# A streaming encoder layer by fast products of seven: weight sums on VectorE instead of adding DMA, and smoother steps

## The chip, the cores and the metric

One core of a Trainium2 chip. The metric is device time in microseconds; before the change the median of three runs is 2205.09 us (2199.73 to 2208.75).

## The reference

One layer (float32), for a prompt of 512 frames and a sample of 32 frames, which share all weights; the kernel runs them as T = 544 columns.

```python
mod = silu(c) @ w_ada + b_ada                       # shift, scale, gate
h = rmsnorm(x, norm_g) * (1 + scale) + shift        # (T, 2048)
z = h @ w_in                                        # w_in (2048, 15360): 120 blocks of 128 columns
au, av, ag, lx, lg, hq, hf, hi, hg, mg = split(z)   # 8 blocks each, mg 48
ya = gmlp_mix(gelu(au), rmsnorm(gelu(av)), ws, bs) * silu(ag)   # gMLP
yb = rglru(causal_conv(lx)) * silu(lg)              # RG-LRU: gates, exp/sqrt, scan over time
yc = rmsnorm(hgrn2_scan(silu(hq), k(hf), logf(hf), hi)) * silu(hg)  # 8 heads, 128 x 128 states
out = (sig(mg0) * (ya @ wb0) + sig(mg1) * (yb @ wb1) + sig(mg2) * (yc @ wb2)) @ w_out
y = rmsnorm(x + gate * out, final_g)
```

Outputs are y and the new states of the convolution, the RG-LRU and the HGRN2 branch, and the v rows of the sample.

## The kernel before

**Products.** `z = h @ w_in` takes pairs of column blocks (b1, b2). Contraction and tokens are halved, and with the two blocks each pair is a 2 x 2 x 2 product, done by seven products instead of eight (`Group`, L330). The operands of the tokens, X1 to X7, are made once; the sums of the weights are made for each pair. Each product is an *item*: 24 matmuls of 128 x 128 by 272 columns, since each float32 weight tile is split in a high and a low part (`halved`, L308; `split`, L230: ScalarE copies to float32r, `wh`, VectorE subtracts, `wl`) and so are the tokens. 60 groups make 420 items, in the order of `todo` (L1169): four of v rows, then the 16 `head` pairs each with a `light` one (mg) behind, four light, then 16 `heavy` ones (eight gMLP, eight RG-LRU) with a light one after each four.

**Order and weight sums.** A group's products interleave with the next one's: 2, 6, 1', 5, 7', 3, 4 (a dash is the next group). Four banks of PSUM: `a` (two, alternating) and `c` (two); product 2 uses the other `a`. Of weights, b1 is halved as p0, p1 and b2 as r0, r1. Products 1, 2 and 3 use p0, p1 and r1 as loaded. Product 5 uses p0 + r0: p0 is loaded a second time and r0 is added by a DMA (`accum_op`, `load_adds`, L261). Product 7 uses q = r0 + r1, loaded and added the same way; VectorE then adds p0 for product 6 (L365), and p1 for product 4.

**Queues.** SyncE loads 512 KB tiles into rings (`raw` five, `q` two, and at the start `early` two), at most nine items ahead (`feed`, L1404). GpSimd issues the adding DMA, spills to DRAM and reloads, and computes some of the head's elementwise work. The program order is the order written by the loop at L1408: item i+2 is prepared (split, sums), item i is multiplied, its PSUM copied out, then `pump` (L453) lets each background generator take one step. A `yield` is thus one item. Every engine works through its own queue in order.

**Background.** Results are put in DRAM (`put_away`, L1122). A head (`hg_gen`, L731) runs when its four blocks are there: gates, exponentials of differences at six levels (GpSimd subtracts L789, ScalarE exponentiates, VectorE multiplies L804 and L875, TensorE multiplies L815 and L885), then states, output and norm. The first one calls `hg_setup` (L710, masks by DMA), the first RG-LRU block `lru_setup` (L1018). `y_gen` (L1191) reloads ya for the stage that follows, `merges` (L1304). Buffers of all these come from one arena, and a buffer is written again only when its last transfer has landed.

Of the kernel before, what the change touches and what calls it, by code (L numbers as in the profile page):

```python
# [42 lines left out]
RAWS = 5  # L43
# [63 lines left out]
def hybrid_step_kernel(ctx: ExitStack, tc: tile.TileContext, xT, cT, w_first, w_in, w_branch, w_out,  # L107
# [139 lines left out]
    items, loads, qloads, adds = [], [], [], []  # L247
# [6 lines left out]
    def item(prep, mul, post=None, pre=None):  # L254
        items.append((prep, mul, post, pre, len(loads), len(qloads)))

    def add(k, n, src):

        adds.append((k, n, src))

    def load_adds(i, last):  # L261

        for e in sorted(adds, key=lambda e: e[0]):
            k, n, src = e
            if k <= i and n in raws:
                nc.gpsimd.dma_start(out=raws[n], in_=src, accum_op=OP.add)  # L266
                adds.remove(e)

    at = {"load": 0, "q": 0}
    EARLY = 34  # L270
    RING = {"raw": RAWS, "early": 2, "q": 2}
# [13 lines left out]
    def load_some(upto):  # L285
        while at["load"] < min(upto, len(loads)):
            n = at["load"]
            ring = "raw"
            if n < START and n % 5 == 1:
                ring = "q"  # L290
            elif "early" in pools.open_ and n < EARLY and n % 5 == 0:
# [6 lines left out]
    def load_q(upto):  # L298
        while at["q"] < min(upto, len(qloads)):
            if at["load"] < START or not free_in("q"):  # L300
                return
            load(("q", at["q"]), qloads[at["q"]], "q", 1024)
            at["q"] += 1
# [26 lines left out]
    class Group:  # L330
# [4 lines left out]
        def __init__(self, n, b1, b2, post, posts=None):  # L335
            self.n, self.b, self.post, self.posts = n, (b1, b2), post, posts or {}
            self.w, self.raw = {}, {}
# [4 lines left out]
        def add(self, i):  # L342

            b1, b2 = self.b
            k = len(items)
            if i == 7:
                self.q = ("q", len(qloads))
                qloads.append(w_half(b2, 0))
                add(k - 5, self.q, w_half(b2, 1))
                n = self.q  # L350
            elif i in (6, 4):
                n = self.q
            else:
                n = need({1: w_half(b1, 0), 2: w_half(b1, 1), 3: w_half(b2, 1), 5: w_half(b1, 0)}[i])
                if i == 5:
                    add(k - 5, n, w_half(b2, 0))
                else:
                    self.raw[i] = n

            def prep():  # L360
                assert not any(e[1] == n for e in adds)
                self.w[i] = halved(raws[n])
                if i in (7, 6):
                    m = self.raw[1 if i == 7 else 2]
                    tt(raws[n], raws[n], raws[m], op=OP.add)  # L365
                    done[m] = True
                elif i not in (1, 2):
                    done[n] = True
# [5 lines left out]
            def after():  # L374
# [4 lines left out]
                elif i == 2:  # L379
                    self.o1 = buf()  # L380
                    tt(self.o1.ap[:, :HF], banks[self.a2], self.u1.ap, op=OP.add)
# [328 lines left out]
    def hg_setup():  # L710
# [19 lines left out]

    def hg_gen(h):  # L731
        if h == 0:
            hg_setup()
# [6 lines left out]
        nc.gpsimd.memset(qb.ap[:, 0:1], 0.0)  # L740
        yield
        yield
# [98 lines left out]
        yield  # L841
        p1, p2 = lev_mm(16), lev_mm(8)
# [9 lines left out]
        lev_w(2)  # L852
        yield
# [29 lines left out]
        nc.vector.tensor_copy(ew[:, 4:5], eq.ap[:, T:T + 1])  # L883
        p1 = lev_mm(1)
        mm(p1[:NS, 272:273], ke.ap[:, NP:], qb.ap[:, T:T + 1], start=True, stop=True)  # L885
        xs[0].free()
        zi = hbuf()
        nc.gpsimd.dma_start(out=zi.ap, in_=scratch[f"hi {h}"])
# [48 lines left out]
        nc.sync.dma_start(out=s0.ap[:, :128], in_=S0[:, h, :])  # L937
# [48 lines left out]
        newton(r, m, t)  # L986
        osb = hbuf(256)
# [6 lines left out]
        qe.free()  # L994
        yield
# [22 lines left out]
    def lru_setup():  # L1018
# [4 lines left out]
        tt(e, e, x, op=OP.min)  # L1023
        act(e, e, AF.Exp)
        ts(u2, e, 2.0, None, op0=OP.add)
# [4 lines left out]
        for n in (17, 15, 13, 11, 9, 7, 5, 3, 1):  # L1030
            tt(acc, acc, u2, op=OP.mult)
            ts(acc, acc, 1.0 / n, None, op0=OP.add)
        tt(acc, acc, u, op=OP.mult)
# [5 lines left out]
    def lru_post(b):  # L1039
# [6 lines left out]
        def post(x, lg):  # L1046
            if b == 0:
                lru_setup()
            start(lru_gen(b, x, lg, w[0]))
# [69 lines left out]
    def z_groups():  # L1119
        av = [(B_AV + j, B_AV + j + 1, av_post(j)) for j in range(0, 8, 2)]  # L1120

        def put_away(n, o, on=None):  # L1122

            if n[:2] in ("hq", "hg"):
                yield
# [14 lines left out]
        def keep(*names, on=None):  # L1140
            def post(*os):
                for n, o in zip(names, os):
                    g = put_away(n, o, on if n == names[-1] else None)
                    if n[:2] in ("hq", "hg"):
                        start(g)
                    else:
                        next(g)
# [21 lines left out]
        todo = av  # L1169
        for i in range(16):  # L1170
            todo += [head[i], light[i]]
        todo += light[16:20]
        rest = iter(light[20:])
        for i, (b1, b2, post, at_start) in enumerate(heavy):
            todo.append((b1, b2, post, {1: at_start}))
            if i % 4 == 3:
                todo.append(next(rest))
        todo += rest
        todo[-1] += ({1: lambda: start(y_gen(0, (1, 2), 0)), 2: lambda: start(y_gen(0, (1, 2), 1))},)
        groups = [Group(n, *t) for n, t in enumerate(todo)]  # L1180
        groups[0].add(1)
        groups[0].add(7)
        for n, g in enumerate(groups):
            nxt = groups[n + 1] if n + 1 < len(groups) else None
            for i in (2, 6, -1, 5, -7, 3, 4):
                if i > 0:
                    g.add(i)
                elif nxt:
                    nxt.add(-i)

    def y_gen(br, pair, h=None):  # L1191

        step = 4 if h is None else 8
        for k in range(0, 8, step):
# [6 lines left out]
            yield  # L1201
            for i, b in enumerate(bs_):
# [6 lines left out]
                if h is None or i == 3:  # L1209
# [186 lines left out]
    with tc.manual_schedule():  # L1396
# [7 lines left out]
        def feed(i):  # L1404
            load_some(items[min(i + 9, len(items) - 1)][4])
            load_q(items[min(i + 6, len(items) - 1)][5])

        for i, (_, mul, post, pre, _, _) in enumerate(items):  # L1408
            feed(i)
            load_adds(i, i + AHEAD)  # L1410
# [94 lines left out]
```

## Time and profile before

| | |
|---|---|
| median of three runs | 2205.09 us |
| profiled execution | 2206.34 us, span 2204.6 us |
| PE, PEld (weight load) busy | 2041.6 us (93%), 1945.3 us (88%) |
| DVE, ACT, POOL busy | 1282.3 (58%), 1103.0 (50%), 503.4 us (23%) |
| DMA | 412.22 MB, HBM read 363.77 MB |
| mean granted TensorE clock | 0.956 |

PE is TensorE, DVE VectorE, ACT ScalarE, POOL GpSimd, SP SyncE. Busy is the time in which an instruction runs; matmuls overlap, so one of 128 x 272 is given 295 ns although the next may start much earlier. A line number is that of the kernel; L190, L232 and L324 are helpers that many places call, and are told apart by the tile's name (`pm` the group products, `px` others, `pp` the products after).

### The profile page before, as it was taken

The page shows a single profiled execution, that of the slowest core. Times are in us where ns is not written, and L with a number is a line of the kernel's source. Part 1 is how long each engine was busy: PE and PEld are TensorE (multiplying, and loading weights), DVE is VectorE, ACT ScalarE, POOL GpSimd, SP SyncE. Part 2 cuts the span into 40 slices and gives each one's busy share as a digit, 9 for nine tenths or more (in the row PEclk, how much of TensorE's full clock was granted, in tenths as well). Part 3 has the DMA queues.
Part 4 walks back from the last instruction along what each step waited for, and adds up shares of the span by engine and source line. Part 5 has one row for each costly group of instructions (what it writes and reads, how often), then busy time and mean ns, then how long its engine had stood idle before and what let it go on. Part 6 is the DMA issues. An engine that isn't in the chain of part 4 may idle for free.

```text
span 2204.6 us, 40701 instructions
## 1 busy us (share of the span) xinstructions
PE 2041.6 (93%) x15864; PEld 1945.3 (88%) x15864; DVE 1282.3 (58%) x2204; ACT 1103.0 (50%) x2137; POOL 503.4 (23%) x720
## 2 busy tenths in 40 slices
PE   5789998989998989898999999999987999999997
PEld 3279988989898989897989999999887999999996
DVE  3365665665766575856575766678675433442226
ACT  3357544655555555554554656567565433332223
POOL 0002122232313141313133222112223222220112
PEclk8789998989999999998999999999999999999998
DMA  8977675756665666665667777666655667665554
GB/s 313 365 190 189 187 187 150 189 158 180 168 187 159 179 165 182 162 190 146 188 161 203 188 198 199 180 156 171 166 147 192 232 185 185 195 196 173 174 173 168
DMA packets 135009, 412.22 MB, mean 187 GB/s; under 512 B 16128, under 2 KB 38432, under 8 KB 134816
## 3 DMA queue, kind: packets, MB, share of 16 engines
q1 hardware_dynamic: 87408, 261.08, 35.3%
q0 software_dynamic: 41424, 138.34, 27.7%
q10 hardware_dynamic: 5984, 10.19, 1.5%
q8 instruction: 125, 2.05, 0.4%
q14 instruction: 68, 0.56, 0.1%
HBM read 363.77 MB, written 45.78 MB: 186 GB/s over the span
## 4 chain that ended last, share of the span: by engine, by line
PE 70%; DMA 8%; DVE 7%; issue 6%; ACT 6%; POOL 2%; DVEq 0%; SPq 0%; ACTq 0%; POOLq 0%
PE pm L324 41%; PE pp L324 21%; DMA q<-in_w_in_dram 3%; ACT arena L190 2%; DVE wl L232 2%; ACT wh L190 2%; PE px L815 1%; DMA d_mg<-arena 1%; PE px L1286 1%; PE px L498 1%; PE px L571 1%; DMA raw<-in_w_ss_dram 1%; DVE x L232 1%; POOL arena L789 1%; DMA arena<-d_hf 1%
## 5 line engine op out<-in xcount | busy, mean ns | idle before, releaser
L324 PE MATMUL pm<-x,wh 128*128 128x272 f32 x6720 | 1316.8, 295 | 49.2 <-ACT arena L190 22.6
L324 PEld LDWEIGHTS pm<-x,wh 128*128 128x128 f32 x6720 | 1088.8, 194 | 58.3 <-ACT arena L190 25.0
L324 PE MATMUL pm<-x,wl 128*128 128x272 f32 x3360 | 987.1, 294 | 2.4 <-DVE wl L232 2.4
L232 DVE TENSOR_TENSOR wl<-raw,wh 128x512 fp32r<-128x512 f32 x652 | 458.1, 729 | 385.0 <-ACT wh L190 381.4
L324 PEld LDWEIGHTS pm<-x,wl 128*128 128x128 f32 x3360 | 649.2, 193 | 4.4 <-DVE wl L232 4.2
L190 ACT ACTIVATE wh<-raw 128x512 fp32r<-128x512 f32 x652 | 391.4, 624 | 334.3 <-PE pm L324 238.3
L324 PE MATMUL pp<-x,wh 128*128 128x272 f32 x2560 | 487.6, 290 | 5.9 <-ACT x L190 2.6
L324 PEld LDWEIGHTS pp<-x,wh 128*128 128x128 f32 x2560 | 402.2, 189 | 20.5 <-issue 13.5
L232 DVE TENSOR_TENSOR wl<-q,wh 128x512 fp32r<-128x512 f32 x360 | 256.1, 737 | 225.9 <-ACT wh L190 224.6
L324 PE MATMUL pp<-x,wl 128*128 128x272 f32 x1280 | 369.4, 289 | 0.0
L190 ACT ACTIVATE wh<-q 128x512 fp32r<-128x512 f32 x360 | 215.5, 624 | 137.7 <-PE pm L324 98.7
L190 ACT ACTIVATE arena<-arena 128x544 f32<-128x544 f32 (+5 forms) x310 | 162.8, 554 | 209.5 <-DVE arena L1339 76.7
L324 PEld LDWEIGHTS pp<-x,wl 128*128 128x128 f32 x1280 | 241.4, 189 | 0.2 <-DVE wl L232 0.2
L190 ACT ACTIVATE arena<-pm 128x272 f32<-128x272 f32 x240 | 93.8, 391 | 182.8 <-PE pm L324 139.8
L266 POOL DMA_DIRECT2D q<-in_w_in_dram x60 | 53.5, 892 | 503.4 <-DMA q<-in_w_in_dram 184.0
L365 DVE TENSOR_TENSOR q<-q,raw 128x1024 f32<-128x1024 f32 x120 | 148.7, 1239 | 4.1
L190 ACT ACT_TABLE_LOAD x59 | 75.7, 1283 | 13.1 <-DVE arena L1063 5.3
L266 POOL DMA_DIRECT2D raw<-in_w_in_dram x60 | 54.1, 902 | 107.7 <-DMA raw<-in_w_in_dram 52.2
L789 POOL TENSOR_TENSOR arena<-arena 128x544 f32<-128x544 f32 (+1 forms) x40 | 52.6, 1327 | 60.1 <-PE px L817 18.3
L815 PE MATMUL px<-arena 128*128 128x128 f32 x160 | 32.4, 333 | 26.9 <-DVE arena L804 17.2
L1242 DVE TENSOR_TENSOR arena<-pp,arena 128x544 f32<-128x544 f32 x48 | 34.7, 723 | 37.0 <-PE pp L324 37.0
L1349 POOL TENSOR_TENSOR tail<-tail,arena 128x544 f32<-128x544 f32 (+1 forms) x15 | 18.6, 1242 | 149.5 <-ACT arena L190 149.5
(265 smaller groups left out, 1425.6 us busy)
## 6 DMA issues: line engine op xcount, KB each, us to landing
raw<-in_w_in_dram SPq DMA_DIRECT2D x240, 512.0 KB, 4.7
q<-in_w_in_dram SPq DMA_DIRECT2D x60, 512.0 KB, 5.0
q<-in_w_in_dram POOLq DMA_DIRECT2D x60, 512.0 KB, 6.3
raw<-in_w_in_dram POOLq DMA_DIRECT2D x60, 512.0 KB, 7.4
raw<-in_w_branch_dram SPq DMA_DIRECT2D x48, 512.0 KB, 4.1
raw<-in_w_ss_dram SPq DMA_DIRECT2D x44, 512.0 KB, 7.0
raw<-in_w_out_dram SPq DMA_DIRECT2D x38, 512.0 KB, 4.6
raw<-in_w_gate_dram SPq DMA_DIRECT2D x32, 512.0 KB, 4.6
```

The source lines that it names most:

```text
L190: return nc.scalar.activation(out, in_, func, **kw)
L232: tt(lo, src, hi.bitcast(F32), op=OP.subtract)
L266: nc.gpsimd.dma_start(out=raws[n], in_=src, accum_op=OP.add)
L324: mm(p, a, rhs(k, r), start=start and i == 0 and q == 0, stop=stop and i == n - 1 and q == 2, **kw)
L365: tt(raws[n], raws[n], raws[m], op=OP.add)
L498: mm(st["xss"][h][:, :HF], ones, st["sq"][q % 2][:, i, h * HF:(h + 1) * HF], start=q == 0 and i == 0, stop=q == 7 and i == 1)
L571: mm(p[32 * i:32 * i + 2, part * 256:part * 256 + 256], cs[:, 4 * q + i, :], w[:, i * 256:(i + 1) * 256], start=q == 0, stop=q == 3)
L789: ptt(v, fv(src, 0, [[2 * m, nb], [m - 1, 2], [1, m]]), fv(src, m - 1, [[2 * m, nb], [0, 2], [0, m]]), op=OP.subtract)
L815: mm(fv(p, 64 * i, [[128, 2], [1, 64]]), x[:, 256 * i + 128:256 * i + 256], fv(x, 256 * i, [[256 + m, 2], [2 * m, nb], [1, m]]), start=Tru ...
L1242: tt(two(g.ap), halves(p), two(g.ap), op=OP.mult)
L1286: mm(p[32 * i:32 * i + 2, :256], cs[:, 4 * q + i, :], w[:, i * 256:(i + 1) * 256], start=q == 0, stop=q == 3)
L1349: ptt(a[:, n], a[:, n], b.ap[:, n], op=OP.add)
```

## The change

Each pair loads p0, p1, r0, r1 once. VectorE makes q = r0 + r1 (`sum_q`), q + p0, then q + p1 in place in one q buffer, and p0 + r0 in place of r0 (`sum_p`). The ring `raw` gets six buffers and `q` one. The adding DMA and `load_q` are gone. The order is 7, 6, 1', 5, 2', 3, 4, and product 2 uses bank `c`. `hg_setup` starts with the first `light` group and `lru_setup` with the last one ahead of the heavy ones, both with more steps; in a head steps are added, the loads of the next head are issued in the last part of this one, and S0 is loaded from GpSimd's queue; `put_away` waits a step. Two `head` groups come first, nine light ones stand together before the heavy ones, and one after them.

```diff
-RAWS = 5
+RAWS = 6
-    RING = {"raw": RAWS, "early": 2, "q": 2}
+    RING = {"raw": RAWS, "early": 2, "q": 1}
...
-            self.a, self.a2, self.c = n % 2, (n + 1) % 2, 2 + n % 2
-            self.bank = {1: self.a, 6: self.a, 5: self.a, 3: self.a, 2: self.a2, 7: self.c, 4: self.c}
+            self.a, self.c = n % 2, 2 + n % 2
+            self.bank = {1: self.a, 6: self.a, 5: self.a, 3: self.a, 2: self.c, 7: self.c, 4: self.c}
+        def sum_q(self):
+            self.q = wp.tile([128, 1024], F32, tag="q", name="q", bufs=RING["q"])
+            tt(self.q, raws[self.raw[5]], raws[self.raw[3]], op=OP.add)
+        def add(self, i, on=None):
             b1, b2 = self.b
+            if i in (1, 2):
+                self.raw[i] = need(w_half(b1, i - 1))
+            elif i == 7:
+                self.raw[5] = need(w_half(b2, 0))
+                self.raw[3] = need(w_half(b2, 1))
             def prep():
+                self.w[i] = halved(self.q if i in (7, 6, 4) else raws[self.raw[i]])
                 if i in (7, 6):
+                    tt(self.q, self.q, raws[self.raw[1 if i == 7 else 2]], op=OP.add)
+                    if i == 6:
+                        done[self.raw[2]] = True
+                elif i in (5, 3):
+                    done[self.raw[i]] = True
+                if on:
+                    on()
+            def sum_p():
+                p = raws[self.raw[5]]
+                tt(p, p, raws[self.raw[1]], op=OP.add)
+                done[self.raw[1]] = True
...
         nc.gpsimd.dma_start(out=t.ap, in_=consts[:, 130:130 + len(LEVELS) * 256])
+        for _ in range(3):
+            yield
         nc.vector.tensor_copy(masks.rearrange("p a e n -> p (a e n)"), t.ap)
...
         lev_w(16)
         lev_w(8)
         yield
+        yield
         p1, p2 = lev_mm(16), lev_mm(8)
...
         yield
+        yield
         p1, p2 = lev_mm(4), lev_mm(2)
...
+        zi = hbuf()
+        nc.gpsimd.dma_start(out=zi.ap, in_=scratch[f"hi {h}"])
+        yield
         p1 = lev_mm(1)
...
-        nc.sync.dma_start(out=s0.ap[:, :128], in_=S0[:, h, :])
+        nc.gpsimd.dma_start(out=s0.ap[:, :128], in_=S0[:, h, :])
...
         newton(r, m, t)
+        yield
...
+        if heads["ready"] > h + 1:
+            hg_load(h + 1)
...
-            for i in (2, 6, -1, 5, -7, 3, 4):
+            for i in (7, 6, -1, 5, -2, 3, 4):
                 if i > 0:
-                    g.add(i)
+                    late = g.sum_p if i == 6 and not nxt else None
+                    g.add(i, late or (nxt.sum_q if i == 4 and nxt else None))
                 elif nxt:
-                    nxt.add(-i)
+                    nxt.add(-i, g.sum_p if i == -1 else None)
...
+            for _ in range(1 if h else 3):
+                yield
...
-                if h is None or i == 3:
+                if h is None or i == 3 or h == 0 and i % 2:
```

## Rows read from the trace of the kernel before

**Rows 1.** The page, part 1: busy time, share of the span, instructions.

```profile
PE 2041.6 (93%) x15864; PEld 1945.3 (88%) x15864; DVE 1282.3 (58%) x2204; ACT 1103.0 (50%) x2137; POOL 503.4 (23%) x720
```

**Rows 2.** Busy time by stage; columns in the first line.

```profile
core 0: us, PE busy (x) PEld busy (x) DVE busy (x) ACT busy (x) POOL busy (x), PEclk, DMA share, GB/s
0.00:124.10 124.10, 76.64 (x640) 36.47 (x640) 45.57 (x91) 47.06 (x76) 1.47 (x6) 0.78 0.87 332
124.10:154.50 30.40, 25.87 (x169) 25.11 (x170) 23.49 (x34) 15.91 (x29) 2.70 (x4) 0.82 0.62 150
154.50:319.60 165.10, 157.20 (x1218) 156.04 (x1217) 95.63 (x157) 100.08 (x236) 25.92 (x40) 0.97 0.69 188
319.60:1185.30 865.70, 809.10 (x6198) 782.51 (x6197) 553.79 (x944) 466.01 (x951) 245.05 (x328) 0.96 0.63 172
1185.30:1430.40 245.10, 244.69 (x1935) 242.75 (x1934) 168.16 (x270) 137.91 (x238) 61.97 (x99) 1.00 0.72 193
1430.40:1631.60 201.20, 187.36 (x1403) 183.93 (x1402) 156.62 (x283) 128.59 (x222) 40.46 (x87) 0.97 0.61 163
1631.60:1672.80 41.20, 28.66 (x178) 26.93 (x177) 27.30 (x53) 26.11 (x51) 9.84 (x24) 0.83 0.47 144
...
```

**Rows 3.** Busy time of undisturbed groups: light; RG-LRU; three of the last head.

```profile
1297.20:1318.30 21.10, 21.10 (x170) 21.10 (x169) 13.56 (x22) 9.33 (x18) 8.14 (x13) 1.00 0.79 224
1460.60:1483.50 22.90, 22.90 (x179) 22.58 (x178) 20.11 (x35) 17.71 (x31) 6.84 (x12) 1.00 0.53 155
1133.20:1207.20 74.00, 74.00 (x597) 71.76 (x597) 49.48 (x92) 37.16 (x82) 23.38 (x40) 1.00 0.71 189
```

**Rows 4.** Instructions on px alone, first group of the last head; PE stands first.

```profile
1103.30:1133.20 29.90, 2.78 (x12) 2.22 (x12) 0.55 (x4) 0.00 (x0) 0.89 0.59 158
```

**Rows 5.** TensorE's waits: us in total, times, longest us.

```profile
PE pm L324 <- ACT arena L190: 22.6, 10, 5.7
PE pm L324 <- ACT wh L190: 17.5, 6, 5.1
PE px L815 <- DVE arena L804: 17.2, 7, 4.7
PE px L885 <- DVE arena L875: 15.2, 6, 3.3
PE px L815 <- ACT wh L190: 9.6, 3, 5.9
PE pm L324 <- DVE arena L381: 9.0, 4, 4.4
```

**Rows 6.** Timeline of one head stall: start us, us, instruction [idle before <-releaser].

```profile
335.67 2.27 POOL L789 TENSOR_TENSOR arena<-arena 128x544 f32<-128x544 f32 x2 [5.51 <-DMA d_mg<-arena]
...
336.84 0.75 ACT L190 ACTIVATE arena<-arena 128x272 f32<-128x272 f32 x2 [4.22 <-POOL arena L789]
...
342.61 1.19 PE L815 MATMUL px<-arena 128*128 128x128 f32 x4 [4.73 <-DVE arena L804]
```

**Rows 7.** Timeline: masks, first and last of lru_setup, a PSUM copy.

```profile
310.96 0.83 DVE L719 CAST masks<-arena 128x1280 uint8<-128x1280 f32 x1 [7.14 <-DMA arena<-in_consts_dram]
...
1437.92 0.16 DVE L1022 TENSOR_SCALAR lru_c<-par 128x8 f32<-128x8 f32 x1
...
1443.93 0.17 DVE L1037 TENSOR_SCALAR lru_c<-lru_c 128x8 f32<-128x8 f32 x1
...
1557.76 0.40 ACT L190 ACTIVATE arena<-pm 128x272 f32<-128x272 f32 x1 [7.66 <-DMA d_y<-arena]
```

**Rows 8.** By line: weight copies, adding loads of q, sums (min/median/max ns).

```profile
L190 ACT ACTIVATE wh<-q 128x512 fp32r<-128x512 f32 x360 | 215.5, 624 | 137.7 <-PE pm L324 98.7 <-DMA q<-in_w_in_dram 37.4 <-DVE q L365 1.2
L266 POOL DMA_DIRECT2D q<-in_w_in_dram x60 | 53.5, 892 | 503.4 <-DMA q<-in_w_in_dram 184.0 <-DMA raw<-in_w_in_dram 120.5 <-DVE wl L232 100.3
...
L365 DVE TENSOR_TENSOR q<-q,raw x120: 1224/1225/2080, 135.4 to 1647.8; 128x1024 f32<-128x1024 f32 x120
```

**Rows 9.** DMA issues: line engine op xcount, KB each, us to landing.

```profile
d_mg<-arena POOLq DMA_DIRECT2D x48, 272.0 KB, 6.0
```

More of the change, by code (lines that the diff above doesn't have):

```diff
@@ L244, in spill @@
         return scratch[name]
-    items, loads, qloads, adds = [], [], [], []
+    items, loads = [], []
     done, raws = {}, {}
@@ L254, in item @@
     def item(prep, mul, post=None, pre=None):
[L255 to L269, printed above, removed]
+        items.append((prep, mul, post, pre, len(loads)))
+    at = {"load": 0}
     EARLY = 34
-    RING = {"raw": RAWS, "early": 2, "q": 2}
+    RING = {"raw": RAWS, "early": 2, "q": 1}
     START = 64
@@ L288, in load_some @@
             ring = "raw"
-            if n < START and n % 5 == 1:
+            if n < START and n % 9 == 1:
                 ring = "q"
-            elif "early" in pools.open_ and n < EARLY and n % 5 == 0:
+            elif "early" in pools.open_ and n < EARLY and n % 9 in (0, 5):
                 ring = "early"
@@ L296, in load_some @@
             at["load"] += 1
[L298 to L303, printed above, removed]
     raws_order = {"early": [], "raw": [], "q": []}
@@ L336, in __init__ @@
             self.n, self.b, self.post, self.posts = n, (b1, b2), post, posts or {}
-            self.w, self.raw = {}, {}
-            self.a, self.a2, self.c = n % 2, (n + 1) % 2, 2 + n % 2
-            self.bank = {1: self.a, 6: self.a, 5: self.a, 3: self.a, 2: self.a2, 7: self.c, 4: self.c}
-        def add(self, i):
-            b1, b2 = self.b
[L345 to L358, printed above, removed]
+            self.w, self.raw, self.next = {}, {}, None
@@ L740, in hg_gen @@
         nc.gpsimd.memset(qb.ap[:, 0:1], 0.0)
+        hg["in", h] = zf, kb, qb
+    def hg_gen(h):
+        while "ready" not in hg:
+            yield
+        if ("in", h) not in hg:
+            hg_load(h)
+            yield
+            yield
+            yield
         yield
-        yield
+        zf, kb, qb = hg.pop(("in", h))
         lb, l1, ln1 = (lbt[:, i, h:h + 1] for i in range(1, 4))
@@ L1143, in post @@
                     g = put_away(n, o, on if n == names[-1] else None)
[L1144 to L1147, printed above, removed]
+                    start(g)
             return post
@@ L1168, in z_groups @@
             heavy.append((B_LX + b, B_LG + b, *lru_post(b)))
[L1169 to L1173, printed above, removed]
+        todo = av + head[:2]
+        todo[4] += ({1: lambda: start(hg_setup())},)
+        for i in range(14):
+            todo += [light[i], head[2 + i]]
+        todo += light[14:23]
+        todo[-1] += ({1: lambda: start(lru_setup())},)
+        rest = iter(light[23:])
         for i, (b1, b2, post, at_start) in enumerate(heavy):
-            todo.append((b1, b2, post, {1: at_start}))
-            if i % 4 == 3:
-                todo.append(next(rest))
+            todo.append((b1, b2, post, {6 if i < 8 else 1: at_start}))
         todo += rest
-        todo[-1] += ({1: lambda: start(y_gen(0, (1, 2), 0)), 2: lambda: start(y_gen(0, (1, 2), 1))},)
+        todo[-1] += ({1: lambda: start(y_gen(0, (1, 2), 0)), 6: lambda: start(y_gen(0, (1, 2), 1))},)
         groups = [Group(n, *t) for n, t in enumerate(todo)]
         groups[0].add(1)
-        groups[0].add(7)
+        groups[0].add(2, groups[0].sum_q)
         for n, g in enumerate(groups):
             nxt = groups[n + 1] if n + 1 < len(groups) else None
-            for i in (2, 6, -1, 5, -7, 3, 4):
+            for i in (7, 6, -1, 5, -2, 3, 4):
                 if i > 0:
-                    g.add(i)
+                    late = g.sum_p if i == 6 and not nxt else None
+                    g.add(i, late or (nxt.sum_q if i == 4 and nxt else None))
                 elif nxt:
-                    nxt.add(-i)
+                    nxt.add(-i, g.sum_p if i == -1 else None)
     def y_gen(br, pair, h=None):
@@ L1405, in feed @@
             load_some(items[min(i + 9, len(items) - 1)][4])
-            load_q(items[min(i + 6, len(items) - 1)][5])
-        for i, (_, mul, post, pre, _, _) in enumerate(items):
+        for i, (_, mul, post, pre, _) in enumerate(items):
             feed(i)
-            load_adds(i, i + AHEAD)
             if pre:
```

31 lines of the change are left out of this document (14 added, 17 removed).

## The prediction

> **What bounds the kernel now.** I read the stages first, then single groups, then TensorE's waits, then the timelines around the longest of them. TensorE is the bound: it is busy in 2041.6 us of 2204.6 [rows 1]. A group (one pair of column blocks, seven products of 24 matmuls) that nothing disturbs takes 21.1 us with TensorE busy throughout and the clock at 1.00: 168 matmuls of 125.5 ns; an RG-LRU group takes 22.9 us, as 2 us of the branch's own products come on top [rows 3]. So the question is what each stage loses against these.
>
> - 124.1 to 154.5, the first group: 30.4 - 21.1 = 9.3 us lost [rows 2, 3].
> - 154.5 to 319.6, seven groups: 165.1 - 7 x 21.1 = 17.4 us; four of them transpose rows of v, for which I allow 1.25 us each; 12 lost.
> - 319.6 to 1185.3, 32 groups with the eight heads: 865.7 us. What a head costs undisturbed I take from the last one: its second to fourth group lasted 74.0 us with TensorE busy throughout [rows 3]; its first has 2.8 us of head products [rows 4], so 21.1 + 2.8 = 23.9 undisturbed. A head is 97.9 us, eight are 783; 82 us lost.
> - 1185.3 to 1430.4, eleven groups, eight of them gMLP: TensorE busy 244.7 of 245.1 [rows 2]; nothing lost.
> - 1430.4 to 1631.6, seven RG-LRU groups and a light one: 201.2 - 7 x 22.9 - 21.1 = 20 us lost.
> - 1631.6 to 1672.8, the last group: 41.2 - 22.9 = 18 us lost; early in the stage after it I allow 8 more.
>
> That is 150 us. The waits say how [rows 5]: in the main, TensorE stands before a head product (L815: 17.2 + 9.6 us, L885: 15.2 us), because VectorE or ScalarE is late, or before a group product because ScalarE is late with a PSUM or weight copy (22.6 + 17.5 us). After the longer ones the granted clock falls from 2.4 to 1.2 GHz and the next matmuls are slow: the heads' stage has a mean clock of 0.96 [rows 2], so 0.04 x 865.7 = 35 us of clock are missing, 2.2 us for each of the 16 waits at head products.
>
> The first lateness is mostly a queue that waits for a transfer. In one head stall GpSimd waits 5.51 us for a spill of mg to land, ScalarE then 4.22 us for GpSimd, and TensorE 4.73 us for VectorE [rows 6]. GpSimd is where the adding loads are issued: those of q alone had 503.4 us of idle queue before them, 184.0 of it for the q load to land [rows 8]. With them in its queue a spill takes 6.0 us from issue to landing [rows 9].
>
> **The change part by part.** *Sums.* Two adding loads per group leave GpSimd's queue (120 issues of some 0.89 us [rows 8], 107 us of an engine that is no bound) with the waits before them, and three 512 KB loads of seven go. The transfers are at a share of 0.63 in the heads' stage [rows 2], so fewer bytes alone I cost at nothing. VectorE gets two more additions of 128 x 1024 per group. The trace has that shape at L365 with 1.224 us at least, 1.225 in the middle, 2.080 at most [rows 8]; both inputs from SBUF as here. I take 1.225: 2.45 us per group, 147 us in all. A gain is excluded, as the addition ran on the transfer before. TensorE hides it where VectorE has room:
>  light group: 13.6 + 2.45 = 16.0 of 21.1 us [rows 3]: hidden;
>  gMLP: 168.2 + 27 = 195 of 245 us [rows 2]: I put 1 us;
>  heads: 553.8 + 78 = 632 of 783 us [rows 2]: hidden on average, not in bursts;
>  RG-LRU: 20.1 + 2.45 = 22.6 of 22.9 us [rows 3]: no room left.
> The new waits: ScalarE's copies of q (products 7, 6, 4) and of the summed p (product 5) now wait for an addition on VectorE. Behind them on ScalarE stand the PSUM copies that products 5 and 3 wait for. One copy takes 0.62 us [rows 8]; if VectorE idles for it after each of the four sums, an RG-LRU group is 22.6 + 4 x 0.62 = 25.1 us. Bounds 22.9 and 25.1; I take 24.5, nearer the upper, as VectorE is full: 8 x 1.6 = +13 us. In the other groups weights are prepared two products ahead, and 16.0 + 2.5 us still lies under 21.1.
>
> For GpSimd's rivalry with VectorE the row comes first: the 120 additions of L365 have a median only 1 ns over their minimum, and the worst is 0.86 us longer [rows 8]; 120 more then cost some microseconds in all. The Trainium skill, "SBUF — State Buffer", section "Who interferes with whom", speaks against the change: a VectorE instruction with two SBUF inputs and a GpSimd instruction that reads SBUF block each other for a whole instruction. By that, were each of the 120 to meet one, they would cost up to 120 x 0.86 = 103 us of VectorE; by the row the sum stays.
>
> *Order of products (7,6,1',5,2',3,4).* Product 2 now goes to the bank of 7, with two products before 7 overwrites it, where one stood before: this frees the wait on L381 (9.0 us [rows 5]), counted in the stages below. The first group begins with 1 and 2, which need no sum; before, its second product waited for an adding load. Of 9.3 us lost, -4.
>
> *Set-ups.* In the heads' set-up VectorE waits 7.14 us for the masks, with the weight copies behind it [rows 7]; now three products lie between. -8, slow clock included, and -2 for spills that land sooner. The RG-LRU set-up is a run of small VectorE instructions from 1437.92 to 1444.1 [rows 7]; cut up, and before the branch: -7.
>
> *Heads.* An extra product, 3 us, stands before three of the five head product pairs (L842, L854, L884), one before the first of the final scaling, and the d_hi load goes a step ahead. Of the L815 and L885 waits, the longest 4.7, 5.9 and 3.3 us [rows 5], 3 us each hides nearly all, if VectorE is as late as now. It is 2.45 us per group later, but GpSimd is earlier, no longer behind landings. Bounds: nothing gained (0) and all but 5 us (-77). I take -52, near two thirds: the waits shrink below what drops the clock. The S0 load, moved from SP to GpSimd, adds eight issues there, by the nearest row 0.89 us each [rows 8], hidden. A head gets 31 steps for 28 and the first starts two groups sooner, so they end about where the gMLP groups begin.
>
> *RG-LRU and end.* -7 (set-up), -6 where ScalarE waited 7.66 us for a y spill to land [rows 7], -5 for the stage's other gaps, +13 from above: -5. The spills' own delay of one step I cost at nothing: they land during later products; a buffer taken again too early costs one such wait. The reload of y in the last group falls beside a light group and in smaller steps: of 18 + 8 us, -18. The first 124 us are bound by transfers (share 0.87, 332 GB/s [rows 2]) with nine load buffers as before: 0.
>
> Sum: -4 - 10 - 52 + 1 - 5 - 18 = -88 us. The profiled execution took 2206.34 us, 1.25 over the median of the three runs. 2206.3 - 88 = 2118 us.
>
> **Rivals.**
> *The head stalls move.* The chain GpSimd, ScalarE, VectorE stays as late as now, held by arena buffers whose spill has not landed, and the sums take what the extra step gives: heads -15 for -52. 2155 us. For it: the 5.51 us wait [rows 6] is for a buffer, not for an adding load. Against: the landing is slow beside these loads.
> *All goes.* Heads -77, the RG-LRU groups stay at 22.9: -13 more. 2206 - 88 - 25 - 13 = 2080 us. For it: gMLP groups run without a gap already.
> *VectorE becomes the bound: slower.* Place: RG-LRU groups at 25.1 us (8 x 2.2 = +18, less 7 for the set-up), and each head's densest group, where 2.45 us of sums and ScalarE behind them push PSUM copies past their two products: 8 x (2.45 + 2.2 of slow clock) = +37. It decides from the point where VectorE's work in a group exceeds TensorE's. With -4, -10 and -10 from the rest: +24, 2230 us. For it: 22.6 of 22.9. Against: only eight groups are that dense.
> *The sums do what the transfers did.* Each wait on a landing becomes one on VectorE, and the steps hide only that: 2206 us.
>
> **How the numbers follow.** Forecast 0.45 (its own range 2095 to 2145), stalls move 0.25, all goes 0.13, VectorE bound 0.12, no change 0.05. A measurement of this kernel can tell about 0.5%, 11 us, from no change. Faster: 0.45 + 0.25 + 0.13 less 0.02 for the moved stalls' upper end: 0.81; same 0.05 + 0.02 + 0.01: 0.08; slower 0.11. The range leaves out the slower case and the lower tail of the fastest: 2072 to 2205.
>
> **What would show it.** No adding load on GpSimd, 240 additions of 1024 columns on VectorE near 1.23 us; VectorE busy some 1430 us; spills landing in well under 6 us; L815 and L885 under 10 us of wait together; gMLP groups still without a gap, RG-LRU groups near 24.5; the heads' stage with clock 0.98 or more. Wrong if the heads lose over 60 us still, if RG-LRU groups pass 25.5, or if ScalarE's waits on VectorE sums turn up before TensorE's in light groups.

## The result, and the profile after

| | median (range) of the runs | profiled execution | span |
|---|---|---|---|
| before, run beside it | 2202.41 us (4 runs) | 2206.34 us | 2204.6 us |
| after | 2133.80 us (2131.50 to 2138.74, 4 runs) | 2138.74 us | 2137.0 us |

The ratio is 0.9692, 95% interval 0.9656 to 0.9728: 3.1% faster. The forecast was 2118 us in a range of 2072 to 2205.

Page of the kernel after: part 1, the share of GpSimd's DMA queue (packets, MB), the three groups of sums (busy us, mean ns | idle before), and the spill of mg (us to landing). They answer to [rows 1, 8, 9].

```profile
PE 2015.4 (94%) x15864; PEld 1914.1 (90%) x15864; DVE 1423.6 (67%) x2324; ACT 1092.1 (51%) x2137; POOL 423.2 (20%) x608
...
q0 software_dynamic: 24400, 75.95, 11.2%
...
L339 DVE TENSOR_TENSOR q<-q,raw 128x1024 f32<-128x1024 f32 x120 | 150.3, 1252 | 4.2
...
L349 DVE TENSOR_TENSOR raw<-raw 128x1024 f32<-128x1024 f32 x60 | 78.6, 1310 | 0.0
L325 DVE TENSOR_TENSOR q<-raw 128x1024 f32<-128x1024 f32 x60 | 77.0, 1284 | 2.0
...
d_mg<-arena POOLq DMA_DIRECT2D x48, 272.0 KB, 4.4
```

These rows show that the change did to the engines what it says: 141 us more on VectorE (forecast 147, or 1430 us busy), and a spill lands in 4.4 us for 6.0. TensorE's busy time fell by 26 us with the same 15864 matmuls, since fewer of them ran at the lower of its two clocks (394 for 754; the granted clock was 1.2 GHz during 108 us of the execution for 194).

The stages of the kernel after, as [rows 2] (start, first group, groups 1 to 7, 8 to 43 with the heads, gMLP, RG-LRU, last group, late):

```profile
0.00:118.96 118.96, 71.86 (x641) 32.67 (x641) 45.59 (x92) 46.93 (x76) 0.41 (x5) 0.82 0.91 348
118.96:155.69 36.73, 27.96 (x168) 27.01 (x169) 24.70 (x36) 15.75 (x29) 0.10 (x1) 0.76 0.18 59
155.69:313.55 157.86, 154.12 (x1219) 152.21 (x1217) 112.20 (x172) 101.26 (x240) 18.24 (x30) 1.00 0.38 124
313.55:1220.55 907.00, 878.60 (x6874) 847.61 (x6873) 695.77 (x1130) 499.04 (x1029) 214.11 (x282) 0.99 0.38 121
1220.55:1400.67 180.12, 180.12 (x1426) 178.83 (x1425) 148.32 (x224) 106.83 (x176) 41.92 (x70) 1.00 0.39 124
1400.67:1572.56 171.89, 164.22 (x1235) 158.26 (x1234) 154.75 (x245) 116.25 (x203) 23.84 (x69) 1.00 0.31 100
1572.56:1608.32 35.76, 25.59 (x178) 24.87 (x177) 30.16 (x56) 23.43 (x48) 11.14 (x24) 0.85 0.52 173
1608.32:2137.00 528.68, 512.91 (x4136) 492.70 (x4136) 212.09 (x376) 182.60 (x339) 113.42 (x131) 0.98 0.61 188
```

"Late" is all that stands behind the last group. The heads' stage has a clock of 0.99 for 0.96. Undisturbed, groups 8 to 43 would take 35 x 21.1 + 22.5 (the one gMLP group among them) + 8 x 13.5 for the head products (97.9 - 4 x 21.1 [rows 3, 4]) = 869 us, so 38 us are lost there where 82 were. The first group has become slower, 36.7 us for 30.4.

TensorE's waits in the kernel after (us, times, longest), against [rows 5]:

```profile
PE pm L305 <- ACT arena L190: 23.2, 13, 7.6
PE pm L305 <- ACT wh L190: 13.4, 9, 4.3
PE pm L305 <- DVE wl L232: 7.9, 17, 1.7
...
PE px L1085 <- DVE arena L1069: 4.0, 5, 0.8
```

The two head products L815 and L885, where TensorE had stood for 42 us, wait no more. Short waits on VectorE's weight parts (wl) have grown, from 2.4 us (5 times). And a kind of wait a step earlier is nearly new (1.2 us before, at L365 [rows 8]); ScalarE in groups 8 to 43:

```profile
ACT wh L190 <- DVE q L325: 66.1, 28, 5.6
...
ACT wh L190 <- DVE raw L349: 57.0, 21, 5.8
ACT wh L190 <- DVE q L339: 53.3, 31, 4.3
```

ScalarE stands 176 us for the three lines of sums. Whether TensorE notices was the point to test.

### The profile page after: what moved, and what is told of

Same layout as the page of the kernel before. It is cut to its first block, busy times and chain, and to the rows that moved or that the text cites. A ratio compares the mean times of both kernels' runs of the same rounds, so it can differ in the third digit from the quotient of the medians.

```text
span 2137.0 us, 40361 instructions
## 1 busy us (share of the span) xinstructions
PE 2015.4 (94%) x15864; PEld 1914.1 (90%) x15864; DVE 1423.6 (67%) x2324; ACT 1092.1 (51%) x2137; POOL 423.2 (20%) x608
## 4 chain that ended last, share of the span: by engine, by line
PE 61%; DVE 8%; issue 5%; ACT 3%; DMA 1%; POOL 1%; DVEq 0%; ACTq 0%; POOLq 0%
PE pm L305 33%; PE pp L305 23%; DVE wl L232 3%; ACT arena L190 2%; ACT wh L190 1%; DVE q L339 1%; PE px L1291 1%; DMA d_hi<-arena 1%; DVE raw L349 1%; PE px L813 1%; PE px L1085 0%; DVE arena L1069 0%; DVE q L325 0%; POOL arena L787 0%; PE px L905 0%
## 5 line engine op out<-in xcount | busy, mean ns | idle before, releaser
L305 PE MATMUL pm<-x,wh 128*128 128x272 f32 x6720 | 1296.6, 292 | 40.8 <-ACT arena L190 23.2
L305 PEld LDWEIGHTS pm<-x,wh 128*128 128x128 f32 x6720 | 1069.2, 191 | 50.8 <-ACT arena L190 26.5
L305 PEld LDWEIGHTS pm<-x,wl 128*128 128x128 f32 x3360 | 638.3, 190 | 15.2 <-DVE wl L232 14.2
L305 PEld LDWEIGHTS pp<-x,wh 128*128 128x128 f32 x2560 | 403.2, 189 | 16.8 <-issue 16.3
L232 DVE TENSOR_TENSOR wl<-q,wh 128x512 fp32r<-128x512 f32 x360 | 248.5, 726 | 101.8 <-ACT wh L190 96.6
L190 ACT ACTIVATE arena<-arena 128x544 f32<-128x544 f32 (+5 forms) x310 | 162.7, 554 | 185.5 <-DVE arena L1344 76.7
L339 DVE TENSOR_TENSOR q<-q,raw 128x1024 f32<-128x1024 f32 x120 | 150.3, 1252 | 4.2
L349 DVE TENSOR_TENSOR raw<-raw 128x1024 f32<-128x1024 f32 x60 | 78.6, 1310 | 0.0
L325 DVE TENSOR_TENSOR q<-raw 128x1024 f32<-128x1024 f32 x60 | 77.0, 1284 | 2.0
L787 POOL TENSOR_TENSOR arena<-arena 128x544 f32<-128x544 f32 (+1 forms) x40 | 63.3, 1601 | 58.1 <-PE px L815 25.2
L1140 POOL DMA_DIRECT2D d_mg<-arena x48 | 26.2, 549 | 199.1 <-DVE arena L378 127.4
L554 PE MATMUL px<-raw,cs 128*2 128x256 f32 x392 | 36.0, 481 | 28.4 <-DVE px L550 21.8
```

Source lines behind the costliest of these rows:

```text
L190: return nc.scalar.activation(out, in_, func, **kw)
L232: tt(lo, src, hi.bitcast(F32), op=OP.subtract)
L305: mm(p, a, rhs(k, r), start=start and i == 0 and q == 0, stop=stop and i == n - 1 and q == 2, **kw)
L325: tt(self.q, raws[self.raw[5]], raws[self.raw[3]], op=OP.add)
L339: tt(self.q, self.q, raws[self.raw[1 if i == 7 else 2]], op=OP.add)
L349: tt(p, p, raws[self.raw[1]], op=OP.add)
```

## The experiments

Twelve kernels ran. The ratio is to executions of the kernel before made beside each (medians 2199 to 2207 us). Stages are from one profiled execution each, as above. That one lies up to 7 us off its kernel's median (e1 6.2 us above it, e7 7.0 us under it), so whole kernels are compared by the ratios. Where the order of the groups is that of before, the stages have other contents, and a star marks them (groups 8 to 43 then hold four gMLP groups, 52 to 58 six RG-LRU and a light one).

| kernel | median us | ratio to before (95%) | first | 1 to 7 | 8 to 43 | RG-LRU | last | late |
|---|---|---|---|---|---|---|---|---|
| before | 2199 to 2207 | 1 | 30.3 | 165.2 | 955.1* | 171.0* | 41.2 | 531.9 |
| after | 2133.80 | 0.9692 (0.9656-0.9728) | 36.7 | 157.9 | 907.0 | 171.9 | 35.8 | 528.7 |
| e1 steps alone | 2110.23 | 0.9592 (0.9576-0.9608) | 30.0 | 158.6 | 896.2 | 163.5 | 34.1 | 525.9 |
| e2 sums alone | 2236.13 | 1.0163 (1.0148-1.0178) | 36.0 | 161.2 | 989.7* | 169.8* | 42.4 | 530.6 |
| e5 e1 + idle sums | 2138.76 | 0.9710 (0.9693-0.9727) | 30.1 | 158.4 | 914.7 | 167.2 | 35.7 | 525.3 |
| e6 sums earlier | 2149.83 | 0.9758 (0.9743-0.9774) | 37.9 | 158.7 | 915.4 | 171.6 | 34.8 | 525.3 |
| e4 a sum on GpSimd | 2196.76 | 0.9983 (0.9970-0.9997) | 38.1 | 162.0 | 950.5 | 180.9 | 36.2 | 526.8 |
| e3 bank, gate step | 2144.05 | 0.9745 (0.9731-0.9760) | 30.2 | 158.1 | 903.9 | 187.2 | 35.0 | 527.8 |
| e10 bank, block later | 2135.94 | 0.9674 (0.9653-0.9696) | 30.6 | 158.2 | 904.3 | 174.5 | 33.6 | 530.2 |
| e9 e1 + xs buffer | 2116.61 | 0.9591 (0.9573-0.9610) | 30.0 | 158.7 | 900.1 | 165.0 | 30.3 | 527.4 |
| e7 e1, no extra products | 2135.79 | 0.9688 (0.9666-0.9710) | 30.1 | 158.2 | 911.9 | 162.8 | 33.7 | 526.2 |
| e11 e7, late loads | 2144.85 | 0.9718 (0.9698-0.9738) | 30.2 | 162.7 | 923.5 | 165.5 | 34.4 | 525.9 |
| e12 e7, spills at once | 2160.30 | 0.9786 (0.9755-0.9817) | 30.2 | 160.4 | 944.0 | 164.4 | 32.1 | 527.4 |
| e13 late spills alone | 2172.10 | 0.9876 (0.9854-0.9898) | 30.0 | 165.0 | 935.3* | 160.5* | 41.4 | 527.9 |

### The two halves of the change: e1 and e2

**e1**: the kernel before with the steps (`hg_setup`, heads, `lru_setup`, `put_away`, order of the groups), its adding loads and order of products kept. **e2**: the kernel before with the sums, loads, rings and order of products, its steps kept.

> The kernel before with the smoother steps alone (set-ups, heads, spills a step later, reload of y, order of the groups); seven loads with adding DMA and the old order of products stay. Theory A (the extra products in front of the head products hide the lateness whatever causes it): the waits of TensorE at the head products fall from 42 us to under 10, the heads' stage loses 45 us at most instead of 82; with set-ups -15 and the end -10 some 2145 us. Theory B (the adding loads in GpSimd's queue cause the lateness, and only their going cures it): the head products still wait over 20 us, the heads lose 65 us or more, some 2175 us.

> The kernel before with the weight sums on VectorE, four loads and the new order of products alone; heads, set-ups, spills and the order of the groups as before. Theory A: the head products still wait for VectorE, over 35 us, and VectorE is later by its sums; RG-LRU groups near 24.6 us; 2200 to 2220 us. Theory B: the head products wait under 20 us, the heads lose 50 us or less; 2165 us or less.

Steps alone, 2110.23 us: with e9 below this is the fastest version, and it beats both kernels. Its stages 8 to 43 and RG-LRU, its waits of TensorE and its spill:

```profile
314.81:1211.06 896.25, 870.88 (x6875) 847.06 (x6873) 618.56 (x1056) 504.18 (x1027) 261.69 (x352) 0.99 0.67 185
...
1391.18:1554.65 163.47, 161.19 (x1234) 158.23 (x1233) 136.52 (x230) 116.71 (x202) 35.05 (x81) 1.00 0.64 170
```

```profile
PE pm L324 <- ACT arena L190: 21.2, 9, 6.0
PE pm L324 <- ACT wh L190: 9.9, 5, 4.4
...
PE pm L324 <- DVE wl L232: 2.4, 6, 0.9
```

```profile
d_mg<-arena POOLq DMA_DIRECT2D x48, 272.0 KB, 6.4
```

No wait at these two head products is left, although the adding loads are all there and a spill still takes 6.4 us; a later one (L951) waits once, 5.2 us. In e2 the spill lands in 4.4 us, and the head products wait as before and longer (L798 and L868 there are L815 and L885):

```profile
PE px L868 <- DVE arena L858: 28.8, 8, 6.3
PE px L798 <- DVE arena L787: 20.3, 7, 3.9
...
PE px L798 <- ACT wh L190: 8.4, 3, 4.0
```

So the steps bring the whole gain and the sums take from it: 1.6% slower alone, 1% on top of the steps (0.9692 against 0.9592, intervals apart). What the faster landings are worth can't be read from e2, where VectorE's sums come with them; that the waits stayed shows that they don't cure these.

### What the sums cost: e5, e6 and e4

**e5** asks whether VectorE's time itself costs, with nobody waiting for the result. To e1 it adds two idle operations per group in the splits of products 5 and 4:

```diff
-                elif i not in (1, 2):
-                    done[n] = True
+                else:
+                    if i in (5, 4):
+                        tt(raws[n], raws[n], raws[n], op=OP.max)
+                    if i not in (1, 2):
+                        done[n] = True
```

> The kernel of the steps alone (2110 us) with two more VectorE operations of 128 x 1024 per group, of the sums' size, on weights that are already used up (the largest of a value and itself, so nothing changes and no copy waits for them). Theory W (the sums cost by VectorE's time): RG-LRU groups rise from 22.9 to some 24.5 us, the heads by 15 to 20 us, some 2135 us, as much as the sums themselves cost. Theory D (they cost because ScalarE's copies wait for them): RG-LRU groups 23.3 us or less, under 2118 us.

Groups 8 to 43 and RG-LRU of e5:

```profile
313.03:1227.69 914.66, 876.67 (x6874) 850.33 (x6873) 707.94 (x1129) 504.65 (x1028) 268.87 (x353) 0.99 0.65 182
...
1407.81:1575.04 167.23, 162.78 (x1235) 158.57 (x1233) 153.68 (x245) 117.35 (x203) 38.10 (x81) 1.00 0.62 167
```

28.5 us over e1 by the medians, 26 by the ratios: as much as the real sums (0.9710 against 0.9692, within each other's intervals), though the adding loads are all there. Between the profiles, 18.4 us of it are in groups 8 to 43, where VectorE's busy time goes from 619 to 708 us. So time on VectorE costs there without any wait on a result (a load buffer also comes free one such operation later, which this run doesn't tell apart). Collisions with GpSimd are not it: VectorE's 89.4 us more are the 72 operations at 1.225 us (88.2), and GpSimd's 40 subtractions in the heads took 1474 ns in the mean for 1420 in e1, 2 us in all. In RG-LRU the idle ones cost 3.7 us and the real ones 8.4; five of seven groups take under 24 us in e5, and one in the kernel after. So there the waits seem to matter too.

**e6** gives the sums one product more of lead (`q` two buffers, `raw` five; p0 + r0 at the split of product 6, r0 + r1 of the next group at that of 3):

> The changed kernel (2134 us) with the same four sums, two of them one product earlier: p0 + r0 behind the split for product 6, r0 + r1 into a second q buffer behind the split for product 3 (raw loads in five buffers to pay for it), so that one other split stands between each of these sums and the copy that reads it. Theory D: ScalarE's wait for these two sums, 119 us in the heads' stage, falls below half, the heads lose 25 us or less instead of 37, RG-LRU groups under 24 us; some 2118 us. Theory W: VectorE has the same work, nothing changes, 2130 us or more.

Groups 8 to 43 took 915.4 for 907.0 and the whole 2149.83 us: with the lead paid for by a load buffer, nothing was gained; what the lead alone would bring, this run doesn't tell. **e4** takes p0 + r0 from VectorE (`tt` becomes `ptt`, GpSimd's):

> The changed kernel with one of the four sums per group (p0 + r0, for product 5) on GpSimd. Theory V (what is left in the heads, 37 us, is ScalarE waiting for sums on a crowded VectorE): VectorE does 74 us less, ScalarE waits less for sums, heads lose 25 us or less, RG-LRU groups 23.7 us or less; some 2115 us. Rival: the sum takes about 2.4 us on GpSimd and stands in its queue before the heads' own work and behind its waits, so product 5 comes late: heads lose 45 us or more, 2140 us or more.

It lost nearly the whole gain. The sum on GpSimd, and VectorE's weight parts and sums (busy, mean ns), in e4:

```profile
L349 POOL TENSOR_TENSOR raw<-raw 128x1024 f32<-128x1024 f32 x60 | 151.1, 2519 | 166.1 <-issue 94.6 <-DVE q L325 71.3
```

```profile
L232 DVE TENSOR_TENSOR wl<-q,wh 128x512 fp32r<-128x512 f32 x360 | 306.1, 886 | 102.2 <-ACT wh L190 99.2 <-PE pm L305 1.5
L339 DVE TENSOR_TENSOR q<-q,raw 128x1024 f32<-128x1024 f32 x120 | 158.0, 1317 | 4.2
```

```profile
PE pm L305 <- DVE wl L232: 28.2, 31, 2.2
```

ScalarE in groups 8 to 43 of e4:

```profile
ACT wh L190 <- DVE q L339: 87.3, 32, 4.9
...
ACT wh L190 <- POOL raw L349: 16.3, 8, 3.7
```

That the sum itself came late is not what cost the time: ScalarE waited 16.3 us for it, 57.0 when VectorE made it. But its waits for the sums left on VectorE grew, at L339 from 53.3 to 87.3 us. VectorE gave up 78.6 us of sums, but the 360 parts of q alone grew from 248.5 to 306.1 us (the mean from 726 to 886 ns, the longest from 1.86 to 3.35 us), and TensorE waited for weight parts 28.2 us for 7.9. All 50 of these parts that took over 0.9 us ran beside a computing instruction of GpSimd's, 37 of them beside the sum; of the 305 under 0.75 us only 38 ran beside any. That is what the Trainium skill says in "SBUF — State Buffer", section "Who interferes with whom": a VectorE instruction with two SBUF inputs and a GpSimd instruction that reads SBUF block each other for a whole instruction. With the sums on VectorE the same rule costs little: their 240 instructions took 305.9 us, 12 more than 240 x 1.225, though GpSimd ran beside them; its 40 subtractions in the heads took 1601 ns in the mean for 1420 in e1, 7 us in all.

### The first group and the RG-LRU stage: e3, e10 and e9

In the kernel after, TensorE in the first group, at its third product:

```profile
138.31 0.79 PE L305 MATMUL pm<-x,wh 128*128 128x272 f32 x2 [4.10 <-DVE arena L364]
```

L364 reads bank `c` of product 2, which product 7 wants to overwrite. Between them there lie two products in every later group (3 and 4 of the group before), and none at the start. **e3** gives the first group's product 2 the other bank, and cuts an RG-LRU block once more:

```diff
-            self.bank = {..., 2: self.c, 7: self.c, 4: self.c}
+            self.bank = {..., 2: self.c if n else 1, 7: self.c, 4: self.c}
...
         x.free()
+        yield
         ri = [[px()[:, :HF] for _ in range(2)] for _ in range(2)]
```

> The changed kernel with one more step in an RG-LRU block ahead of its gate products, and product 2 of the first group alone in a bank of its own. Theory V (VectorE fills an RG-LRU group, 22.8 of 24.7 us): these groups stay at 24.5 us or more. Theory P (the gate products merely stand too early for the convolution on VectorE, 1.0 and 0.7 us of wait per group): they fall to 23.2 us or less, some -11 us. First group: with the bank the 4.1 us wait on the sum of the outputs goes and the slow clock after it, 36.7 us becomes 31 or less. In all 2118 us by P, 2128 us by V.

The bank gives back what the first group had lost: 30.2 us. The step does harm, 27.2 us a group for 24.7. ScalarE in such a group of e3:

```profile
1515.92 0.40 ACT L190 ACTIVATE arena<-pm 128x272 f32<-128x272 f32 x1 [1.39 <-DVE arena L1075]
```

A PSUM copy now waits for the arena buffer that the convolution has only just given back, and TensorE for the copy (1.74 us). **e10** keeps the bank, starts each RG-LRU block a product later instead, and makes its `xs` buffer of two arena units:

> The changed kernel (2134 us) with all its sums on VectorE, and three small edits: product 2 of the first group in a bank of its own, an RG-LRU block that starts one product later, so that its convolution comes behind the four sums and not among them, and the two-unit buffer for its first rows. Theory P (the 24.7 us of these groups come from where the sums stand, as 2.45 us of idle work moved them by only half a microsecond): 23.3 us or less, the first group 30 us, in all 2114 us. Theory V (VectorE is full): 24.5 us or more, 2127 us.

Most RG-LRU groups took 24.8 to 26.9 us, and the whole 2135.94 us, no gain over the kernel after. **e9** is e1 with that `xs` buffer:

> The kernel of the steps alone (2110 us) with the small buffer of the convolution's first rows taken as two units of the arena and not one, so that ScalarE's PSUM copies do not land in a unit that VectorE's convolution has just read. Theory: ScalarE's waits for the convolution (19.6 us) and TensorE's 6.3 us in the last group go with the slow clock after them: the last group falls from 34 to 27 us, in all 2101 us. Rival: the copies take another buffer that is as late, 2110 us as before.

The last group fell to 30.3 us from 34.1, not to 27, and the rest gave it back: 0.9591 against 0.9592 for e1. So with the sums in them most RG-LRU groups stay over 24.5 us in each of the cuts that ran (in e10 all but two of seven); most are at 22.9 in e1, without the sums.

### What the steps are made of: e7, e11, e12 and e13

**e7** is e1 without the three extra products ahead of head products (the three `yield` of L842, L854 and L884, and the d_hi load back in its place). **e11** is e7 without the early loads of the next head (`hg_load` at the end of a head, and the wait ahead of the first). **e12** is e7 with the spills of hf, hi and mg issued at once:

```diff
-            yield
             if n[:2] in ("hq", "hg"):
+                yield
...
-                    start(g)
+                    if n[:2] in ("hq", "hg"):
+                        start(g)
+                    else:
+                        next(g)
```

> The kernel of the steps alone (2110 us) without the three extra products ahead of the head products, and the load of hi again behind the third; all other steps stay. Theory A (these three products hide the lateness): TensorE waits 30 us or more at the head products again, the heads' stage is 40 us longer, some 2150 us. Rival (earlier loads of the head, later spills and the order of the groups do it): under 10 us of wait at the head products, 2110 to 2120 us.

> The kernel of the steps alone without the three extra products (2136 us; 912 us from the ninth group to the 44th), and also without the head's loads ahead of its turn: they are issued in its first step and used two products later, as before the change. If these early loads made the larger part of what the heads gained (39 of 55 us came without the three products), that stretch takes 930 us or more and the whole 2150 us or more; if not, 915 us and 2136 us.

> The kernel of the steps alone without the three extra products (2136 us), and with the spills of mg, hf and hi issued at once as before the change and not one product later. If GpSimd's queue, which then stands before VectorE's last addition of the group, is what makes the heads late, the ninth to 44th group take 930 us or more and the whole 2150 us or more, with GpSimd waiting again for the additions at its spills; if not, 915 us and 2136 us.

Between the profiles, taking away the extra products costs 16 us in groups 8 to 43 (911.9 for 896.2), the early loads 12 (923.5 for 911.9, between the two expectations), the late spills 32 (944.0 for 911.9). By the ratios of the whole it is 21, 7 and 22 us; the 7 are not clear of noise, as the intervals of e7 and e11 overlap. I had costed the late spills at nothing. Without the extra products TensorE waits again at the two head products, 23.7 us in e7, between its two theories:

```profile
PE px L830 <- DVE arena L819: 10.0, 8, 2.4
PE px L900 <- DVE arena L890: 8.0, 5, 2.9
...
PE px L830 <- ACT wh L190: 5.7, 2, 4.7
```

In e12 these waits are 36.8 us, and VectorE stood 25.9 us at additions from PSUM that wanted a buffer whose spill had not landed. That wait is among VectorE's neither in e7 nor before, so part of the 32 us is a price that the kernel before did not pay:

```profile
DVE arena L381 <- DMA d_mg<-arena: 25.9, 5, 7.4
```

**e13** asks the same from the other side: the kernel before with the late spills and nothing else.

```diff
+            yield
             if n[:2] in ("hq", "hg"):
-                yield
...
-                    if n[:2] in ("hq", "hg"):
-                        start(g)
-                    else:
-                        next(g)
+                    start(g)
```

> The kernel before with one edit: the spills of hf, hi and mg are issued one product after their block is complete, as in the changed kernel. Everything else is as before: adding loads, order of the groups, set-ups and steps of the heads. Theory S (the late spill is worth much by itself, as e12 against e7 says): the heads' stage, 865.7 us before, falls by 20 us or more and the time to 2187 or less. Rival C (it is worth that only beside the other steps, since without them TensorE stands before the head products for another lateness): the heads' stage falls by less than 10 us, the time stays at 2195 or more.

26.9 us from spills issued one product later, 1.2% of the time, with as many bytes. The time is on the first theory's side; the heads' stage fell by 19.8 us (865.70 to 845.92), a hair short of its 20. GpSimd in the heads' stage, before and then in e13: its adding loads of q (busy, mean ns | idle before them, and what ended it), and its waits with a spill of mg:

```profile
L266 POOL DMA_DIRECT2D q<-in_w_in_dram x32 | 28.5, 891 | 181.6 <-DMA q<-in_w_in_dram 134.9 <-DVE arena L804 15.6 <-DVE wl L232 14.0
...
POOL d_mg L1134 <- DVE arena L395: 35.5, 14, 5.8
```

```profile
L266 POOL DMA_DIRECT2D q<-in_w_in_dram x32 | 28.5, 891 | 169.0 <-DMA q<-in_w_in_dram 74.2 <-DVE wl L232 43.4 <-DVE q L365 14.0
...
POOL d_mg L1134 <- DVE arena L395: 19.5, 8, 4.2
```

And the heads' and the RG-LRU stage of e13, to be read against 865.70 us with TensorE busy 809.10 and a clock of 0.96 [rows 2], and 171.0 us:

```profile
320.28:1166.20 845.92, 797.32 (x6198) 771.67 (x6197) 556.92 (x944) 465.93 (x952) 251.06 (x328) 0.97 0.63 176
1440.52:1601.04 160.52, 159.26 (x1226) 156.84 (x1225) 133.02 (x222) 114.79 (x197) 35.29 (x76) 1.00 0.63 174
```

A spill issued as its block ends stands at the head of GpSimd's queue until VectorE has finished that block, and everything behind it stands too. Issued one product later it finds its block done more often (8 waits for 14, 19.5 us for 35.5). The idle time before the adding loads fell too, by 12.6 us; the rest of what their rows show is a change of what ended it. The RG-LRU stage gained 10.5 us: ScalarE's waits for a y spill to land went from 12.3 to 1.6 us there, though y spills were not touched, only the other spills in the same queue. What the runs don't show is which single wait of GpSimd's passes on to TensorE; its waits at head products hardly changed (42.0 to 40.9 us), and what fell in the heads' stage is 8 us of TensorE's idle time (56.6 to 48.6) and 12 us of its busy time, that is fewer matmuls at the lower clock. The order of the groups and the set-ups were not run by themselves.

## Why the prediction was right, and where not

The total was right in sign and near in size: 2133.8 for 2118 us, and the likeliest case's own range (2095 to 2145) holds it. The changes by stage, forecast and measured between the two profiled executions:

| step | forecast | measured |
|---|---|---|
| start | 0 | -5.1 |
| first group | -4 | +6.4 |
| set-ups, groups 1 to 7 | -10 | -7.3 |
| heads (lost: 82, then) | -52 (30) | -44 (38) |
| gMLP | +1 | 0 |
| RG-LRU (lost: 20, then 171.9 - 7 x 22.9) | -5 (15) | -8.4 (11.6) |
| last group and late | -18 | -8.6 |
| sum | -88 | -67 |

**First group.** The step that failed: "The first group begins with 1 and 2, which need no sum". True, but product 2 shares its bank with 7, which stands right behind it in this group alone. I counted the two products in between ("with two products before 7 overwrites it") from the running order and did not look at its beginning. e3 and e10, which give it another bank, show the 6 us.

**Sums.** "Hidden on average, not in bursts" was costed at nothing for the heads; there lies the bigger miss in mechanism. e5 shows that such time on VectorE costs 18 us in groups 8 to 43 with nobody waiting for its result, and the kernel after has 10.8 us more there than e1. Of these TensorE's busy time holds 7.7 and its waits 3.0: many short ones (wl, 13 times in this stage, 4 in e1) and not a few long ones. gMLP (180.12 us in both) and groups 1 to 7 hid them, as said. An RG-LRU group came out at 24.7 us, forecast 24.5, the term with a worked-out bound:

```profile
1498.50:1523.20 24.70, 23.55 (x179) 22.65 (x178) 22.85 (x37) 17.53 (x31) 3.23 (x10) 1.00 0.32 102
```

VectorE is busy 22.85 us of it (22.6 in the working). An undisturbed group in e1 takes 22.90 us with TensorE busy throughout. In e5, where VectorE does as many operations and nothing waits for the idle ones, most groups take under 24 us, which speaks for the waits in that bound. One of the seven took 25.6 us, over the mark of 25.5.

**Heads.** The forecast of 30 us lost was near (38; in e1 27), for a reason that I had wrong in part. I gave the whole 52 us to the extra products and to GpSimd being earlier without adding loads. The runs, by the profiles: extra products 16, early loads 12 (not clear of noise), and the spills' delay, "I cost at nothing", 32 beside the other steps and 20 alone. That the forecast came near is in part luck: what the extra products brought less than I gave them, a term that I had put at nothing brought. To end the waits at L815 and L885 the adding loads did not have to go (e1 keeps them and has no such wait; e2 drops them and waits 57.5 us there); the extra products did it (none in e1, 23.7 us in e7). The row that I read was right, GpSimd 5.51 us behind a landing [rows 6], but e13 gains 20 us in this stage by the order in its queue, with the bytes unchanged.

**Set-ups, RG-LRU and end.** Set-ups: right but for 3 us, and e1 has it without the sums (158.6). RG-LRU: the size was near; the waits for spills that land late (-6) did go, but they also go with the adding loads kept (2.4 us in e1, 1.6 in e13, 12.3 before). The last group still waits, 4.55 us for the convolution's buffer, and e9, with another one, is 4 us shorter there than e1. I had taken all of its 18 + 8 us from the y reloads, which was wrong for about half. The start is 119.0 to 123.8 us in the profiles that begin like the kernel after, so 5 us there are no effect that one profile can tell.

**Rivals.** "VectorE becomes the bound" looked for the harm of the sums in the right place, the heads: in e2, with the steps of before, groups 8 to 43 are 35 us longer and the kernel 1.6% slower. The steps outweighed it. But VectorE is not full there (busy 72% of that stage in e2, 77% after), so the condition of this rival was not what decided. "The head stalls move" (2155 us) fell: its two head products wait no more. Of the marks set beforehand, the 42 us at L815 and L885 went under 10, the clock in groups 8 to 43 is 0.99, and gMLP has no gap. One mark of the other kind showed, ScalarE's waits on sums, 176 us in groups 8 to 43, for the most part with no wait of TensorE's behind them: TensorE waited 19.9 us for ScalarE's copies in that stage.

What stays open: which instruction's lateness carries the price of an idle operation (18.4 us for 72 of them in groups 8 to 43, 0.26 us each, with VectorE busy 77% of that stage).

## What to carry to other kernels

When a change has two halves, run each alone: here one brought 4% and the other took 1% of it, and the whole looked like a gain by both. Work moved from a DMA off the path to an engine that is 64% busy is not free because it fits on average; in this kernel 120 operations that nobody waited for cost as much as the additions that were needed. Before removing an instruction from an in-order queue, try to issue the one that blocks it a step later: here that alone gave 1.2%.

## What was not expected of the hardware

An addition of 128 x 1024 in float32 took 2.40 us in the median on GpSimd (2.35 to 2.92) against 1.22 us on VectorE, and beside it VectorE's own two-input instructions took up to 2.3 us longer than in the median (L339: 3.51 us for 1.22; 2.08 at most in the kernel after). So moving 60 of them away left VectorE busier in groups 8 to 43 (720 us for 696). Dropping 180 of 420 weight loads (512 KB each), 120 of them adding ones, shortened the landing of unrelated spills from 6.0 to 4.4 us, and of loads on SyncE's queue from 4.7 to 4.1 us.
